# A hybrid attention and state-space layer: token sums and split output weights in spaced steps, V copies beside the second half's units, unused dense products at the beginning of attention

## The chip, the cores and the metric

The kernel runs on one core of one Trainium2 chip. The time is device time in microseconds (us) of that core; the median of the runs counts. A profiled execution has a time of its own, which stands beside them.

## The reference, cut to what matters

One decoder layer on 2048 tokens of width 1024, all in float32. The input x is projected by one large matrix into q, k, v, two gates z, the state-space branch's xbc and dt. Then come two branches, a concatenation, one output projection and a layer norm:

```
proj = einsum('bsd,de->bse', x, w_in)
q, k, v, z_att, z_ssm, xbc, dt_raw = split(proj, SPLITS)
o1, l1 = dilated_window_attention(q, k, v, slopes, 1)     # 16 heads of 64, window of 128 steps
o2, l2 = dilated_window_attention(q, k, v, slopes, 4)
o3, l3 = dilated_window_attention(q, k, v, slopes, 16)
wts = softmax(stack([l1, l2, l3]))
y_att = rms_norm((wts[0]*o1 + wts[1]*o2 + wts[2]*o3) * silu(z_att), att_norm_g)
xbc = silu(causal_depthwise_conv(xbc, conv_w, conv_b))
dt = softplus(dt_raw + dt_bias)
y = ssd_chunked(xs, dt, -exp(a_log), b, c) + d_skip * xs  # chunks of 128
y_ssm = rms_norm(y * silu(z_ssm), ssm_norm_g)
out = einsum('bse,ed->bsd', concat([y_att, y_ssm]), w_out)
x = layer_norm(alpha * x + out, ln_g, ln_b)
```

## The kernel before, in words

Products in full precision are made of three matmuls in a faster 32-bit format: each operand is split into a high part (a cast, on ACT) and a remainder (a subtraction, on DVE or POOL), and high x high, high x low and low x high are added up in PSUM.

**Stage 1, to about 209 us** (lines 126 to 218): v and dt are projected for all tokens, and x is split. In the same loop the sums of token blocks for the first half of the tokens are made, and the upper eight of the sixteen row blocks of the output weights are split and stored in DRAM (`d_wo`).

**Stage 2, to about 1248 us** (lines 220 to 723): all other projections, by a Strassen-like scheme of seven products where eight would be needed. A *job* makes 256 columns of the projection for one half of the tokens (1024): 10 jobs on the first half (jobs 0 to 9, states and gates of the state-space branch), 22 on the second half (jobs 10 to 31), and 12 on the first half again (jobs 32 to 43, q, k and the attention gate). The order is the list `jobs` (lines 605 to 612). A job is seven *steps*, and a step is one product: twelve matmuls of 128x128 by 512 columns (`mm` in `products`, lines 305 to 352). So there are 308 steps; step 7m + s is step s of job m.

A product needs a token tile and a weight tile. The seven token tiles (`LEFT`, line 85) are blocks of x or sums of blocks; they lie in DRAM as `d_T` and are loaded, when the token half changes, by fourteen transfers of 1 MB on POOL's queue (`token_side`, lines 225 to 236), one tile after each step of the job before, as each old tile comes free. The weight tiles of the next job are made in each job: loads on ACT's queue (`column_load`), sums on DVE (line 258), casts on ACT (line 265), remainders on POOL (line 266). Results leave PSUM by copies on ACT (`keep`, line 319) and additions on DVE (`put`, line 327).

The order on PE, DVE, ACT and POOL is the order of the program (`manual_schedule`, line 650): each of these engines does its instructions one after the other, and an instruction that waits holds up all behind it. SP issues transfers. Work that belongs to no job is put into steps by hand: `later` maps a step's number to functions, `after(n, f)` adds one n steps on, and `flush` runs them after each step's product (lines 294 to 303). Put there are, among others:

- the token sums of the second half (`sums_load`, `sums_part`, lines 95 to 112): for each of four row groups k, two loads of 128x1024 from x, and four parts. A part is one subtraction on DVE (line 108), a cast on ACT (line 110), the remainder on DVE (line 111) and a store on SP's queue (line 112), all in one step. In job 1 + k they stand in steps 1 to 4. The buffers: two `st`, two `to`.
- the lower eight row blocks of the output weights, in halves (`wout_load` and `split_w`, lines 115 to 123 and 654 to 659): sixteen loads on ACT's queue at steps 35 to 55, three steps later the cast on ACT (line 117) and the remainder on DVE (line 118) in one step, two steps later the store on POOL's queue (line 119).
- 32 copies of V from DRAM to DRAM in the order of the two larger dilations (`copy_v`, line 496), on POOL's queue, 512 KB each: 13 at steps 3 to 51, 19 at steps 77 to 149, every fourth step.
- softplus and decays of dt (`decays`, lines 440 to 491), in pieces after jobs 1, 2 and 3; the first of them is a chain of small DVE instructions (lines 453 to 474).
- the convolution (three long DVE instructions per tile, line 416) in jobs 10 to 22, and from step 157 on the 32 units of the state-space scan (lines 503 to 601).

**Stage 3, to about 1765 us** (lines 726 to 1133): attention, eight pairs of heads. A pair has 24 units (three dilations d, four blocks, two halves). A unit is 12 score matmuls with 64 rows (line 816), a fused add-and-minimum on DVE (line 824), exponentials on ACT (line 832), transposes on PE (line 845) copied by DVE (line 847), and value matmuls (line 865). PE does the scores of unit i, the transposes of unit i-2 and the values of unit i-3 in one pass of the loop at line 1079. In the dilation that comes first (d = 0, units 0 to 7) and in the first block of the next (units 8 and 9), a unit has 128 keys for each query block instead of 256. The queries for the other dilations are permuted on POOL (`permute`, lines 773 to 787).

**Stage 4** (lines 1134 to 1181): output projection and layer norm.

Of the kernel before, what the change touches and what calls it, by code (L numbers as in the profile page):

```python
# [9 lines left out]
F32 = mybir.dt.float32  # L10
# [18 lines left out]
def hybrid_layer(ctx, tc, xT, xc, w52, wv, convw, convb, dtb, alog, dskp, gcol, wout,  # L29
# [56 lines left out]
    with ExitStack() as c1:  # L86
# [8 lines left out]
        def sums_load(pool, p, k):  # L95

            r = [pool.tile([128, 1024], F32, name="st", bufs=4 if p == 0 else 2) for _ in range(2)]
            for h in range(2):
                kk = k + 4 * h
                nc.sync.dma_start(r[h], xT[kk * 128:(kk + 1) * 128, p * 1024:(p + 1) * 1024])  # L100
            return r

        def sums_part(pool, p, k, r, c):
# [5 lines left out]
            t = pool.tile([128, 2, 512], F32R, name="to", bufs=6 if p == 0 else 2)  # L109
            nc.scalar.copy(t[:, 0], o)  # L110
            nc.vector.tensor_tensor(t[:, 1], o, t[:, 0].bitcast(F32), op=OP.subtract)
            nc.sync.dma_start(dap(d_T[p, nm], k * 512, [[2048, 128], [128 * 2048, 2], [1, 512]]), t.bitcast(F32))


        def split_w(e, hf, raw, t, store=True):
# [3 lines left out]
            put_w = lambda queue: queue.dma_start(d_wo[e][:, :, hf * 512:hf * 512 + 512], t.bitcast(F32))  # L119
            if store:  # L120
                put_w(nc.sync)
            else:
                after(2, lambda: put_w(nc.gpsimd))


        with tc.tile_pool(name="ts", bufs=1, reuse_waits="tile") as ts, \
# [57 lines left out]
            for pc in range(4):  # L184
# [19 lines left out]
                if 0 < pc < 3:  # L204
                    for k in (2 * pc - 2, 2 * pc - 1):
                        r = sums_load(ts, 0, k)
                        for c in range(4):
                            sums_part(ts, 0, k, r, c)
# [441 lines left out]
        with tc.manual_schedule(engines={E.PE, E.DVE, E.Activation, E.Pool}):  # L650
# [599 lines left out]
```

## Time and profile before

| | us |
|---|---|
| median of 3 runs | 2175.16 |
| lowest, highest run | 2175.14, 2181.51 |
| the profiled execution's own time | 2171.41 |
| its span, first to last instruction | 2169.6 |
| mean granted TensorE clock in it | 0.972 |

A page of the profile lists the busy time of each engine, the granted clock and the DMA load over the span, and groups of instructions by line. Views of the trace answer closer questions: how busy each engine was between two times, who waited for whom, and which instructions ran in a window, with the idle time before each and what ended it. PE is TensorE's matmuls, PEld its weight loads, DVE VectorE, ACT ScalarE, POOL GpSimd, SP SyncE. L310 is line 310 of the kernel. In rows of windows, the columns are: window, its length, then busy time and number of instructions of each engine, then granted clock, mean busy share of the 16 DMA engines, and GB/s. The profile's shares are averages over four unlike stages, so what a part is worth is read from its own stretch.

### The profile page before, as it was taken

Reading aid. Unit: us, or ns where it says so; the run is one execution under the profiler, and the core shown is the slowest. Engines: PE = TensorE matmul, PEld = TensorE weight load, DVE = VectorE, ACT = ScalarE, POOL = GpSimd, SP = SyncE. Lnnn points to the kernel's source line nnn. Section 1 sums busy time; section 2 is a strip of 40 time slices with the busy share of each in tenths; the row PEclk is TensorE's granted clock in tenths of the full one; section 3 lists DMA queues with packets and bytes.
Section 4 is the critical chain, followed back from the end, with each engine's and each line's share of the span. In section 5 each row is a group of like instructions: output and inputs, shape, how many; then the busy total and the mean of one; then the engine's idle time right before and its main releaser. Section 6 shows DMA issues by size and latency. Waiting matters only on the chain.

```text
span 2169.6 us, 38851 instructions
## 1 busy us (share of the span) xinstructions
PE 2048.0 (94%) x13824; PEld 1703.7 (79%) x13824; DVE 1394.1 (64%) x3145; ACT 1154.4 (53%) x3007; POOL 1092.5 (50%) x899
## 2 busy tenths in 40 slices
PE   7999998989999999979999999999999977999998
PEld 7998776768887887858888877888878865888886
DVE  3431554548998677835555468888888845655655
ACT  4231444435565677645676468888888841222221
POOL 2122545657886666755555331776666670422222
PEclk9999999989999999999999979999999988999999
DMA  9999778976678888899888853777876799232220
GB/s 330 370 333 338 234 255 281 326 279 213 204 231 293 310 318 302 296 389 298 269 276 286 302 203 88 217 222 220 245 212 185 213 366 286 95 105 84 96 83 29
DMA packets 260801, 525.26 MB, mean 242 GB/s; under 512 B 43712, under 2 KB 122688, under 8 KB 244608
## 3 DMA queue, kind: packets, MB, share of 16 engines
q1 hardware_dynamic: 181984, 255.37, 36.9%
q0 software_dynamic: 35280, 184.30, 24.1%
q10 hardware_dynamic: 43344, 83.12, 11.7%
q8 instruction: 109, 1.79, 0.3%
q14 instruction: 84, 0.69, 0.1%
HBM read 346.15 MB, written 193.33 MB: 249 GB/s over the span
## 4 chain that ended last, share of the span: by engine, by line
PE 47%; DMA 8%; DVE 5%; ACT 3%; issue 3%; POOL 2%; ACTq 0%; SPq 0%; POOLq 0%; DVEq 0%
PE S L816 7%; PE N L865 7%; PE T L845 6%; PE S L1025 4%; PE S L1027 3%; PE S L1026 3%; PE pp L310 3%; PE pp L314 3%; PE pp L312 3%; PE T L1025 2%; PE T L1026 2%; PE T L1027 2%; DMA TT3l<-d_T0T 1%; DVE P L824 1%; ACT P L832 1%
## 5 line engine op out<-in xcount | busy, mean ns | idle before, releaser
L266 POOL TENSOR_TENSOR w<-wr,w 128x512 fp32r<-128x512 f32 x231 | 357.2, 1562 | 177.5 <-ACT w L265 146.5
L832 ACT ACTIVATE P<-P,st 128x256 f32<-128x256 f32 (+1 forms) x768 | 345.1, 451 | 96.6 <-DVE st L824 96.2
L824 DVE CUSTOM_DVE_ANT_0 P<-S,tb 128x256 f32<-128x256 f32 (+1 forms) x768 | 235.4, 362 | 81.3 <-PE S L816 47.2
L319 ACT COPY ev<-pp 128x512 f32<-128x512 f32 x176 | 102.2, 581 | 184.9 <-PE pp L314 123.4
L847 DVE COPY PT<-T 128x512 f32<-128x512 f32 (+1 forms) x304 | 196.5, 677 | 1.3 <-PE T L845 1.3
L845 PE MATMUL T<-ident,P 128*128 128x128 f32 x1200 | 178.8, 286 | 6.0 <-DVE PT L847 6.0
L865 PE MATMUL N<-PT,v 128*64 128x128 f32 x2400 | 176.5, 284 | 0.0
L265 ACT CAST w<-wr 128x512 fp32r<-128x512 f32 x231 | 137.9, 618 | 52.5 <-DVE wr L258 35.8
L865 PEld LDWEIGHTS N<-PT,v 128*64 128x64 f32 x2400 | 129.2, 138 | 33.2 <-issue 22.6
L258 DVE TENSOR_TENSOR wr<-wr 128x512 f32<-128x512 f32 x132 | 145.0, 1099 | 15.6 <-DMA wr<-w 12.5
L845 PEld LDWEIGHTS T<-ident,P 128*128 128x128 f32 x1200 | 129.8, 142 | 30.3 <-DVE PT L847 7.4
L932 POOL TENSOR_TENSOR wb<-num,wb 128x2048 f32<-128x2048 f32 x21 | 96.4, 4591 | 98.1 <-ACT P L832 57.8
L832 ACT ACTIVATION_READ_ACCUMULATOR P<-P,st 128x1 f32 x768 | 143.9, 187 | 0.0
L327 DVE TENSOR_TENSOR ev<-pp,ev 128x512 f32<-128x512 f32 x152 | 100.6, 682 | 53.5 <-PE pp L314 45.2
L816 PE MATMUL S<-kh,qp 64*128 64x256 f32 (+1 forms) x1024 | 126.6, 306 | 0.0
L1002 DVE TENSOR_REDUCE tb<-P 128x128 f32<-128x1024 f32 x32 | 64.0, 2000 | 85.2 <-PE N L1031 49.2
L416 DVE SCALAR_TENSOR_TENSOR acc<-U,cw,acc 128x2048 f32<-128x2048 f32 x36 | 105.2, 2922 | 3.2 <-ACT acc L413 2.8
L816 PEld LDWEIGHTS S<-kh,qp 64*128 64x128 f32 x1024 | 88.9, 188 | 22.0 <-issue 20.9
L367 DVE SCALAR_TENSOR_TENSOR ev<-ev 128x512 f32<-128x512 f32 x64 | 64.2, 1015 | 64.3 <-ACT ev L366 64.2
L150 PE MATMUL pp<-vh,xh 128*128 128x256 f32 (+1 forms) x320 | 90.2, 289 | 15.4 <-ACT xh L173 15.4
L143 POOL TENSOR_TENSOR vl<-vraw,vh 128x256 fp32r<-128x256 f32 (+1 forms) x32 | 29.7, 933 | 130.5 <-ACT vh L142 125.7
L1064 POOL TENSOR_TENSOR kh<-kh,wb 128x1024 f32<-128x1024 f32 x8 | 19.2, 2398 | 142.6 <-DVE kh L1063 142.6
(368 smaller groups left out, 6135.2 us busy)
## 6 DMA issues: line engine op xcount, KB each, us to landing
wr<-w ACTq DMA_DIRECT2D x157, 256.0 KB
v<-d_v POOLq DMA_DIRECT2D x24, 1024.0 KB, 7.0
wb<-d_wd SPq DMA_DIRECT2D x48, 512.0 KB
d_wc<-w SPq DMA_DIRECT2D x44, 512.0 KB
w<-d_wc POOLq DMA_DIRECT2D x44, 512.0 KB, 6.2
csb<-d_cs ACTq DMA_DIRECT2D x32, 512.0 KB
st<-xT SPq DMA_DIRECT2D x31, 512.0 KB
d_v<-vt SPq DMA_DIRECT2D x16, 512.0 KB
```

Source lines behind the costliest of these rows:

```text
L258: tt = lambda o, a, b, op=OP.subtract: nc.vector.tensor_tensor(q[o], q[a], q[b], op=op)
L265: nc.scalar.copy(t[:, 0], q[nm])
L266: nc.gpsimd.tensor_tensor(t[:, 1], q[nm], t[:, 0].bitcast(F32), op=OP.subtract)
L816: nc.tensor.matmul(ov(sp[h][:, 256 * b:256 * b + w]), A["q"][d][x][hr, blk], kv(A["k"][y][hr]), start=(m == 0), stop=(m == 2))
L824: nc.vector.tensor_tensor_reduce(P[:, h, b, 256 - w:256], sp[h][:, c0:c0 + w], tab[:, h, tab.shape[2] - w:], 1.0, 3.0e38, OP.add, OP.min, ...
L832: nc.scalar.activation(p, p, AF.Exp, bias=stat(A, 0, d, h, blk), scale=-1.0, accum_out=stat(A, 1, d, h, blk))
L845: nc.tensor.transpose(tp[:, h, b], P[:, h, b, 128 * which:128 * which + 128], ident)
L847: nc.vector.tensor_copy(pt[:, :, bl[0]:2], tp[:, :, bl[0]:2])
L865: nc.tensor.matmul(nm[64 * h:64 * h + 64, bq * 128:bq * 128 + 128], v[:, k, 64 * h:64 * h + 64], pts[which][:, h, b], start=(f or not whic ...
L1025: nc.tensor.matmul(ps, uh[:, e, :], wh, start=(e == 0), stop=False)
L1026: nc.tensor.matmul(ps, uh[:, e, :], wl, start=False, stop=False)
L1027: nc.tensor.matmul(ps, ul[:, e, :], wh, start=False, stop=(e == 7))
```

## The change

- Token sums of the second half: `sums_load` and `sums_part` keep only stage 1's use. A new `token_sums(k, b)` puts every single operation into a step of its own: for group k, with b = 7 + 8k, four loads of 128x512 at steps b-7, b-3, b-2 and b, and for part c the subtraction at b + 2c, the cast at b + 2c + 1, the remainder and the store at b + 2c + 2. The buffers: five `st` of half the size, two `to`. The last store is at step 39, and the pool is closed after job 5 instead of job 4.
- Split output weights: `w_steps` puts load, cast, remainder and store of each of the sixteen halves at steps c, c + 3, c + 4 and c + 5, with c from 42 to 62. The queues are the same. `woraw` has four buffers instead of three.
- The 32 copies of V stand at steps 73, 76, ... 166, every third step.
- `warm`: after the scores of each of the first four units of attention, eight matmuls of 128x128 by 512 columns on a tile of k, into a PSUM tile of the transposes' ring. Nothing reads the result.

```diff
-        def sums_load(pool, p, k):
+        def sums_load(pool, k):
...
+        put = lambda n, f: later.setdefault(n, []).append(f)
+
+        def token_sums(k, b):
+            R = {}
+            def load(nm, h, q):
+                R[nm] = sums.tile([128, 512], F32, name="st", bufs=5)
+                kk = k + 4 * h
+                nc.sync.dma_start(R[nm], xT[kk * 128:(kk + 1) * 128, 1024 + 512 * q:1536 + 512 * q])
+            for n, x in ((-7, ("11", 0, 0)), (-3, ("12", 0, 1)), (-2, ("22", 1, 1)), (0, ("21", 1, 0))):
+                put(max(b + n, 0), lambda x=x: load(*x))
+            for c, (nm, o, a, d) in enumerate((("T1", "11", "12", "11"), ("T3", "12", "22", "12"),
+                                               ("T2", "22", "22", "11"), ("T4", "21", "22", "21"))):
+                t = []
+                def high(o=o, t=t):
+                    t.append(sums.tile([128, 2, 512], F32R, name="to", bufs=2))
+                    nc.scalar.copy(t[0][:, 0], R[o])
+                def low(o=o, t=t, nm=nm):
+                    nc.vector.tensor_tensor(t[0][:, 1], R[o], t[0][:, 0].bitcast(F32), op=OP.subtract)
+                    nc.sync.dma_start(dap(d_T[1, nm], k * 512, [[2048, 128], [128 * 2048, 2], [1, 512]]),
+                                      t[0].bitcast(F32))
+                put(b + 2 * c, lambda o=o, a=a, d=d: nc.vector.tensor_tensor(R[o], R[a], R[d], op=OP.subtract))
+                put(b + 2 * c + 1, high)
+                put(b + 2 * c + 2, low)
...
-            put_w = lambda queue: queue.dma_start(d_wo[e][:, :, hf * 512:hf * 512 + 512], t.bitcast(F32))
-            if store:
-                put_w(nc.sync)
-            else:
-                after(2, lambda: put_w(nc.gpsimd))
+            nc.sync.dma_start(d_wo[e][:, :, hf * 512:hf * 512 + 512], t.bitcast(F32))
+        def w_steps(e, hf, c):
+            R = []
+            g = gc[:, e:e + 1]
+            def load():
+                R.append(sums.tile([128, 512], F32, name="woraw", bufs=4))
+                nc.scalar.dma_start(R[0], wout[e * 128:e * 128 + 128, hf * 512:hf * 512 + 512])
+            def high():
+                R.append(sums.tile([128, 2, 512], F32R, name="wot", bufs=4))
+                nc.scalar.activation(R[1][:, 0], R[0], AF.Copy, scale=g)
+            def low():
+                nc.vector.scalar_tensor_tensor(R[1][:, 1], R[0], g, R[1][:, 0].bitcast(F32), op0=OP.mult,
+                                               op1=OP.subtract)
+            def store():
+                nc.gpsimd.dma_start(d_wo[e][:, :, hf * 512:hf * 512 + 512], R[1].bitcast(F32))
+            for n, f in ((0, load), (3, high), (4, low), (5, store)):
+                put(c + n, f)
...
-            def wout_load(j):
-                raw = sums.tile([128, 512], F32, name="woraw", bufs=3)
-                nc.scalar.dma_start(raw, wout[j // 2 * 128:j // 2 * 128 + 128, j % 2 * 512:j % 2 * 512 + 512])
-                after(3, lambda: split_w(j // 2, j % 2, raw, sums.tile([128, 2, 512], F32R, name="wot", bufs=4), False))
             for j in range(16):
-                later.setdefault(35 + 4 * j // 3, []).append(lambda j=j: wout_load(16 + j))
+                w_steps(8 + j // 2, j % 2, 42 + 4 * j // 3)
+            for k in range(4):
+                token_sums(k, 7 + 8 * k)
             for j in range(32):
-                later.setdefault(4 * j + (3 if j < 13 else 25), []).append(lambda j=j: copy_v(1 + j // 16, j % 16))
+                put(73 + 3 * j, lambda j=j: copy_v(1 + j // 16, j % 16))
...
-            raws = {0: sums_load(sums, 1, 0)}
...
-                if 1 <= m < 5:
-                    for c in range(4):
-                        after(1 + c, lambda c=c, k=m - 1: sums_part(sums, 1, k, raws[k], c))
-                    if m < 4:
-                        after(5, lambda k=m: raws.__setitem__(k, sums_load(sums, 1, k)))
...
-                if m == 4:
+                if m == 5:
                     sub.close()
...
+        def warm(A):
+            ps = psT.tile([128, 512], F32, name="T")
+            x = A["k"][0]
+            for n in range(8):
+                nc.tensor.matmul(ps, x[:, 0, :], x[:, 4:8, :].rearrange("p r j -> p (r j)"), start=True, stop=True)
...
                     pts[i] = scores(pairs[pr], d, qd, half)
+                    if i < 4:
+                        warm(pairs[0])
```

More of the change, by code (lines that the diff above doesn't have):

```diff
@@ L93, in hybrid_layer, with sums_part @@
         dsk = sm.tile([128, 8], F32, name="dsk")
-        def sums_load(pool, p, k):
-            r = [pool.tile([128, 1024], F32, name="st", bufs=4 if p == 0 else 2) for _ in range(2)]
+        def sums_load(pool, k):
+            r = [pool.tile([128, 1024], F32, name="st", bufs=4) for _ in range(2)]
             for h in range(2):
                 kk = k + 4 * h
-                nc.sync.dma_start(r[h], xT[kk * 128:(kk + 1) * 128, p * 1024:(p + 1) * 1024])
+                nc.sync.dma_start(r[h], xT[kk * 128:(kk + 1) * 128, 0:1024])
             return r
-        def sums_part(pool, p, k, r, c):
+        def sums_part(pool, k, r, c):
             b11, b12, b21, b22 = r[0][:, 0:512], r[0][:, 512:1024], r[1][:, 0:512], r[1][:, 512:1024]
@@ L205, in hybrid_layer @@
                     for k in (2 * pc - 2, 2 * pc - 1):
-                        r = sums_load(ts, 0, k)
+                        r = sums_load(ts, k)
                         for c in range(4):
-                            sums_part(ts, 0, k, r, c)
+                            sums_part(ts, k, r, c)
                 if pc in (1, 2):
```

6 lines of the change are left out of this document (3 added, 3 removed).

## Prediction

> **What bounds the kernel now.** The page first: PE is busy for almost the whole span, so time is gained only where PE stands still or runs slowly. Steps and jobs are counted as in the section on the kernel. The stretches below are cut at the start of job 0, of job 10 (the change of token half), of jobs 11, 22 and 23, of attention, and of its pair 1.
>
> ```profile
> span 2169.6 us, 38851 instructions
> PE 2048.0 (94%) x13824; PEld 1703.7 (79%) x13824; DVE 1394.1 (64%) x3145; ACT 1154.4 (53%) x3007; POOL 1092.5 (50%) x899
> ```
> ```profile
> core 0: us, PE busy (x) PEld busy (x) DVE busy (x) ACT busy (x) POOL busy (x), PEclk, DMA share, GB/s
> 209.40:428.90 219.50, 200.42 (x847) 162.83 (x848) 124.94 (x158) 98.63 (x172) 122.87 (x120) 0.95 0.80 271
> 428.90:466.70 37.80, 26.44 (x86) 18.92 (x85) 5.61 (x10) 7.59 (x12) 15.28 (x19) 0.82 1.01 379
> 466.70:679.00 212.30, 211.08 (x926) 172.99 (x925) 195.90 (x144) 121.58 (x194) 172.41 (x135) 1.00 0.69 215
> 679.00:706.40 27.40, 22.44 (x86) 17.65 (x85) 22.26 (x19) 12.84 (x21) 14.45 (x8) 0.88 0.92 318
> ...
> 1248.40:1319.90 71.50, 68.63 (x676) 55.57 (x675) 50.73 (x227) 51.69 (x203) 23.51 (x37) 0.81 0.47 165
> ```
>
> The same view for line 310 alone, which has four matmuls in a step, dates the losses of the first half:
>
> ```profile
> 209.40:263.20 53.80, 30.17 (x76) 14.72 (x77) 0.97 0.81 261
> 263.20:282.20 19.00, 5.88 (x12) 2.80 (x13) 0.82 0.62 213
> ...
> 312.40:331.90 19.50, 8.49 (x20) 3.99 (x19) 0.91 0.64 227
> 331.90:356.50 24.60, 14.13 (x36) 6.93 (x37) 1.00 0.78 254
> 356.50:404.40 47.90, 22.97 (x57) 10.89 (x57) 0.93 0.86 297
> ```
>
> Nine undisturbed steps take 24.6 us, so a fed step costs 2.73 us (and one of its 12 products 0.228). The 70 steps of jobs 0 to 9 would then take 191.3; they take 219.5, 28.2 more. The second row has 3 steps in 19.0 (10.8 lost), the third 5 in 19.5 (5.8), the last 14 in 47.9 (9.7); the first, 19 in 53.8, loses 1.9, most of it the very first weight tile. Job 10 loses 37.8 - 19.1 = 18.7, jobs 11 to 21 lose 212.3 - 210.4 = 1.9, job 22 loses 8.3.
>
> Who stops PE in jobs 0 to 9? The view of waits names ACT's copies out of PSUM. The timeline of ACT (brackets: idle before, and what ended it) and of DVE shows what stood in front of these copies:
>
> ```profile
> PE pp L310 <- ACT ev L319: 18.6, 6, 7.6
> ```
> ```profile
> 268.18 0.62 ACT L110 CAST to<-st 128x512 fp32r<-128x512 f32 x1 [8.27 <-DVE st L108]
> 272.62 0.62 ACT L110 CAST to<-st 128x512 fp32r<-128x512 f32 x1 [3.30 <-DVE st L108]
> 273.14 0.58 ACT L319 COPY ev<-pp 128x512 f32<-128x512 f32 x1
> ...
> 299.67 0.62 ACT L110 CAST to<-st 128x512 fp32r<-128x512 f32 x1 [5.31 <-DMA d_T1T<-to]
> 325.54 0.62 ACT L110 CAST to<-st 128x512 fp32r<-128x512 f32 x1 [7.23 <-DMA d_T1T<-to]
> 370.26 0.72 ACT L117 ACTIVATE wot<-woraw,gc 128x512 fp32r<-128x512 f32 x1 [3.73 <-DMA d_wo<-wot]
> ```
> ```profile
> 252.24 0.41 DVE L453 TENSOR_TENSOR xr<-xr,dtbt 128x256 f32<-128x256 f32 x1
> 267.12 0.43 DVE L474 TENSOR_TENSOR adt<-dts,al 128x256 f32<-128x256 f32 x1
> 267.46 0.68 DVE L108 TENSOR_TENSOR st<-st 128x512 f32<-128x512 f32 x1
> ```
>
> ACT works in order. In the first two rows its cast of a token sum waits for a subtraction that stands on DVE behind the whole softplus chain (252.2 to 267.5); in the two casts of line 110 that follow it waits until an older sum has been stored; in the last row until an older split weight has been stored. These are the places that the spaced steps touch.
>
> **The change, part by part.**
>
> *Token sums and weights (jobs 0 to 9).* The number of casts, subtractions and stores is the same. What moves is the distance: subtraction, cast, remainder and store were in one step, now they stand one step (2.73 us) apart, and a sum's buffer is taken again three steps after its store was issued. The 13 V copies of these steps go away. Stretch by stretch: the softplus chain stays on DVE, begun after step 13 as now. The cast of group 1 at step 16 still waits for the subtraction of step 15, which comes after 267.5 plus one remainder and itself, 1.4, so at about 268.9; then cast, one weight cast, and ACT copies for PE at about 270.3, where now the copy begins only at 273.1 because a second cast sat in front of it. I keep 6 of the 10.8. The waits for stores should nearly go (1 of 5.8 kept), and of the weights' 9.7 I keep 1.8, since cast and remainder no longer wait on each other back to back. Saving 4.8 + 4.8 + 7.9 = **17.5 us**. Bounds: 8 (only the weights' part) and 24 (all but the first tile and 2 us).
>
> A remainder risk is DVE itself:
>
> ```profile
> 306.29 5.90 DVE L108 TENSOR_TENSOR st<-st 128x512 f32<-128x512 f32 x1
> 306.60 5.03 POOL L266 TENSOR_TENSOR w<-wr,w 128x512 fp32r<-128x512 f32 x4
> ```
>
> One subtraction of usually 0.68 lasted 5.90 while POOL ran four tensor operations beside it. The Trainium skill (SBUF — State Buffer, Who interferes with whom) says that a VectorE instruction with two SBUF inputs and a GpSimd instruction that reads SBUF lock each other out; the trace agrees, and by that rule a distance of one step does not cover such a block.
>
> *The reload of the second half (job 10).* Split weights are now loaded at steps 42 to 62 and stored on POOL's queue five steps later, at 47 to 67. The fourteen 1 MB loads of job 10's token tiles are issued on the same queue from step 63 on. Until now the last store was issued at 409.0, ahead of them:
>
> ```profile
> L119 POOL DMA_DIRECT2D d_wo<-wot x16: 677/695/822, 348.7 to 409.0; - x16
> d_wo<-wot POOLq DMA_DIRECT2D x16, 512.0 KB, 6.5
> q0 software_dynamic: 35280, 184.30, 24.1%
> L496 POOL DMA_DIRECT2D d_v<-d_v x32: 514/572/835, 224.2 to 676.8; - x32
> ```
>
> Job 10 is bound by these transfers (DMA share 1.01, 379 GB/s). Four stores (steps 63, 64, 65, 67) now lie among them: 4 x 0.524 MB at 379 GB/s is **+5.5 us**; bounds 0 and 10 (the upper one also for the convolution's first buffers, which now take the memory of weight buffers whose stores lie in that queue). Two V copies (73, 76) queue behind the loads and cost job 10 nothing, at most 3.
>
> *V copies.* From queue 0, 184.3 MB took 24.1% of 2169.6 us, so a copy of 0.524 MB takes 1.5 us of all 16 DMA engines, and 0.6 us of POOL to issue. Behind a copy on POOL stand the weight remainders (line 266) that PE needs one job later. In jobs 11 to 21 there are 25 copies for 19: 9 us of DMA on a stretch with share 0.69, 3.6 us of POOL where 40 of 212 are free. I take +1, bounds 0 and 5. The last five (154 to 166) fall into jobs 22 and 23, where no copy was, where the DMA share is 0.92 already and ACT waits for stores of its own results:
>
> ```profile
> 688.34 0.58 ACT L319 COPY ev<-pp 128x512 f32<-128x512 f32 x1 [4.52 <-DMA d_kh<-ev]
> ```
>
> Five copies are 7.5 us of DMA; I take **+3**, bounds 0 and 8.
>
> *Unused products at the start of attention.* Pair 0 takes 71.5 us with a clock of 0.81. The score matmuls (12 to a unit) and then all engines:
>
> ```profile
> 1258.80:1280.20 21.40, 9.26 (x72) 8.13 (x72) 0.50 0.20 74
> 1328.30:1342.20 13.90, 6.19 (x84) 5.21 (x84) 1.00 0.36 96
> 1248.40:1258.80 10.40, 7.53 (x65) 5.92 (x64) 6.31 (x36) 8.57 (x34) 10.00 (x15) 0.78 1.00 342
> 1258.80:1280.20 21.40, 21.40 (x146) 16.78 (x144) 9.75 (x54) 11.70 (x53) 2.44 (x5) 0.50 0.20 74
> 1258.96 2.28 POOL L784 CAST qp<-ql 128x512 fp32r<-128x512 f32 x4
> ```
>
> Units 4 to 9 take 3.57 us each at half clock, the same units of pair 1 1.99 at full clock: 6 x 1.58 = 9.5, and unit 10 another 0.5. DMA is nearly idle, and POOL is done with the permuted queries at 1261.2, so nothing else is late there. The price: 32 products of 0.228 are 7.3 us on PE in the first four units, where PE has 10.4 - 7.5 = 2.9 idle; those units get rid of their own half-clock part (clock 0.78 over 10.4 us is 4.6 us at half, so 2.3). So +2.1, and in all **-7.9**; bounds -10 and +12 (below). That the clock stays granted I take from pair 1: the same small products keep full clock there once it is granted, and the clock is lost in pair 0 while PE waits. The Trainium skill (TensorE: Matmul & The Clock Gate, Part 1) says that one busy window of about 3.4 us brings full clock. By that, units 4 to 10 would be fast already and this part would cost 2.1 instead of saving 7.9. The trace disagrees: 21.4 us without a gap at 0.50. So the rule gets no share of the chances.
>
> **Sum.** -17.5 + 5.5 + 1 + 3 - 7.9 = -15.9. The profiled execution's own time is 2171.4 (span 2169.6 and 1.8 around it), 3.8 under the median 2175.2 of the runs; it becomes 2155.5, the median **2159.3**.
>
> **Rivals.** (1) *The clock falls all the same*, because the gaps between the four groups are too long. Then 32 products cost 0.456 each, 14.6 - 2.9 = +11.7 for -7.9: 2159.3 + 19.6 = 2178.9, no change. For it: four small groups with waits between. Against: each group is denser than anything in that stretch. 8%.
> (2) *Spacing buys little*: the chain on DVE and SP's late stores delay the casts at any distance that short, and only 4 of 17.5 come: 2172.8, no change. For it: 8.27 of the waits has the softplus chain behind it, which stays. Against: 9.7 us hang on weights, far from that chain. 11%.
> (3) *Slower: POOL is held by its own queue.* Issuing there can stop until an older transfer has landed:
>
> ```profile
> 433.67 0.53 POOL L233 DMA_DIRECT2D TT4l<-d_T1T  x1 [3.91 <-DMA TT1l<-d_T1T]
> ```
>
> Were each of the 30 copies from job 11 on held so for 3 us, POOL would stand 90 us, and it has 53 free in jobs 11 to 22 (239.7 less 172.4 and 14.5): 37 us late on weights, 2159.3 + 37 = 2196. It decides once eight transfers are outstanding on POOL's queue when a copy is issued (in this row T4's load waits for the one eight places ahead of it). Against: there fourteen loads came in a row, now a copy comes every third step, 8.2 us, and takes 1.5 us of transfer. 10%.
> (4) *Better*: with the copies gone, jobs 0 to 9 lose only 4 and jobs 22 and 23 nothing: 2150. 9%.
>
> **Numbers.** Forecast 62%. About 0.3% (6.5 us) is what a measurement of this kernel can tell from no change. Faster: forecast and (4), 0.71. Same: (1) and (2), 0.19. Slower: (3), 0.10. Range 2146 to 2178: below it lies the forecast with nearly all best bounds, above it (1) and (3), 18%.
>
> **What would show it.** Jobs 0 to 9 in about 202 us instead of 219.5, ACT's casts without waits on stores, one remaining stall near step 20. Job 10 at 43 instead of 37.8, all on DMA waits. Jobs 11 to 21 within 214, job 22 near 30. Pair 0 at about 64 us instead of 71.5, with clock 1.00 after 1250. It would be wrong if the stretch 209 to 429 stays over 212, if clock 0.50 stands in pair 0, or if POOL waits for landings at the copies.

## The result, and the profile after

The changed kernel takes 2194.24 us at the median of 6 runs (2186.44 to 2199.24), the kernel before, beside it, 2176.22 (2173.27 to 2181.51): a ratio of 1.0072 [1.0057, 1.0087]. It is slower by 0.7%, where 0.7% faster was forecast, and it lies outside the range. The profiled execution took 2199.24 us, 5 above its median, so its span exaggerates a little: 27.7 us over that of before, where the medians differ by 18.0.

```profile
span 2197.3 us, 38933 instructions
PE 2054.4 (93%) x13856; PEld 1705.9 (78%) x13856; DVE 1395.1 (63%) x3145; ACT 1153.8 (53%) x3007; POOL 1082.2 (49%) x899
```

PE has 6 us more work (the 32 unused products) and 27.7 us more span: what was lost was lost standing or at a lower clock. The busy windows, cut at the same points as before (starts of job 0, 10, 11, 22, 23, 32, then pair 0 of attention), say where:

```profile
core 0: us, PE busy (x) PEld busy (x) DVE busy (x) ACT busy (x) POOL busy (x), PEclk, DMA share, GB/s
210.30:410.70 200.40, 195.17 (x846) 160.59 (x847) 124.76 (x158) 98.00 (x172) 117.36 (x104) 0.98 0.76 252
410.70:453.20 42.50, 27.36 (x85) 18.96 (x84) 5.52 (x10) 7.65 (x12) 19.38 (x25) 0.80 1.04 398
453.20:695.70 242.50, 220.05 (x925) 176.81 (x924) 202.11 (x144) 119.97 (x191) 162.08 (x139) 0.96 0.64 202
695.70:725.50 29.80, 21.11 (x85) 16.68 (x84) 20.47 (x19) 14.50 (x24) 15.05 (x11) 0.89 0.95 316
725.50:960.00 234.50, 222.89 (x1183) 183.39 (x1182) 162.65 (x238) 157.51 (x318) 154.88 (x123) 0.98 0.87 305
1279.68:1347.10 67.42, 65.69 (x708) 53.08 (x707) 50.29 (x227) 51.45 (x203) 23.55 (x37) 0.97 0.49 176
```

Jobs 22 to 31 together, in the same view of the kernel before:

```profile
679.00:929.90 250.90, 240.61 (x1267) 197.81 (x1266) 184.22 (x257) 172.03 (x342) 169.14 (x128) 0.99 0.88 310
```

| stretch | before | after | difference | forecast |
|---|---|---|---|---|
| to job 0 | 209.4 | 210.3 | +0.9 | 0 |
| jobs 0 to 9 | 219.5 | 200.4 | -19.1 | -17.5 |
| job 10 | 37.8 | 42.5 | +4.7 | +5.5 |
| jobs 11 to 21 | 212.3 | 242.5 | **+30.2** | +1 |
| jobs 22 to 31 | 250.9 | 264.3 | **+13.4** | +3 |
| jobs 32 to 43 | 318.5 | 319.6 | +1.1 | 0 |
| pair 0 | 71.5 | 67.4 | -4.1 | -7.9 |
| the rest | 849.7 | 850.2 | +0.5 | 0 |

Two rows hold most of the miss, 39.6 of the 43.6 us between the forecast change of the span (-15.9) and the measured one (+27.7), and both are stretches to which V copies were moved. In jobs 11 to 21 the DMA share fell from 0.69 to 0.64 although there are six copies more: the engines' bandwidth did not run out. POOL is no busier than before (162 us of 242). Something waited. The view of waits for that stretch, lines that bear on the path to PE; first before:

```profile
POOL U L395 <- DMA d_xs<-U: 13.4, 4, 8.1
ACT ev L319 <- POOL w L266: 8.1, 2, 4.9
DVE U L325 <- DMA d_xs<-U: 8.0, 2, 6.2
```

and after (us in total, times, longest; U is line 442, the remainders 313, PE's third product 361):

```profile
ACT ev L366 <- POOL w L313: 31.4, 5, 11.2
DVE U L372 <- DMA d_xs<-U: 21.1, 4, 7.4
POOL U L442 <- DMA d_xs<-U: 18.5, 4, 7.0
PE pp L361 <- POOL w L313: 15.2, 8, 8.9
POOL U L442 <- issue: 12.3, 1, 12.3
PE pp L357 <- ACT ev L366: 7.0, 4, 5.7
ACT ev L366 <- DMA d_ql<-ev: 4.5, 1, 4.5
```

So PE itself waits 15.2 us for remainders of POOL and 7.0 for ACT's copies out of PSUM. `d_xs<-U` is the store of the convolution's results, on SP's queue. There are two buffers U. The load of the next U stands in POOL's queue, and it must wait until the buffer's store has landed. Behind it in POOL's queue stand the weight remainders that PE needs in the next job. One such chain, read from the timelines of SP, POOL, DVE and PE:

```profile
532.09 1.67 SPq L475 DMA_DIRECT2D d_xs<-U  x1
```
```profile
533.11 0.62 POOL L543 DMA_DIRECT2D d_v<-d_v  x1
533.75 2.54 POOL L313 TENSOR_TENSOR w<-wr,w 128x512 fp32r<-128x512 f32 x2
548.61 1.55 POOL L442 DMA_DIRECT2D U<-d_cu  x2 [12.31 <-issue]
...
551.35 2.16 POOL L313 TENSOR_TENSOR w<-wr,w 128x512 fp32r<-128x512 f32 x1
```
```profile
546.46 1.29 DVE L372 TENSOR_TENSOR U<-pp,ev 128x512 f32<-128x512 f32 x2 [7.35 <-DMA d_xs<-U]
```
```profile
553.56 0.80 PE L361 MATMUL pp<-TT2h,w 128*128 128x512 f32 x1 [8.86 <-POOL w L313]
554.16 0.63 PE L357 MATMUL pp<-TT2h,w 128*128 128x512 f32 x1
...
557.57 0.63 PE L361 MATMUL pp<-TT2h,w 128*128 128x512 f32 x1
...
558.93 0.39 PE L357 MATMUL pp<-TB22h,w 128*128 128x512 f32 x1
```

A V copy is issued 1 us after the store. DVE's sum into the buffer is held until 546.46, so the store had taken 14 us; POOL does its first remainder in 15 us at 551.35, and PE stands 8.86 us for it. (The timeline puts POOL's 12.31 us down to "issue"; the view of line 475 counts them among the waits of U's loads for such stores, "POOL U L442: 30.8, 5".) From its issue to the last update of its semaphore in the trace, this store of job 14 takes 14.2 us here and 14.1 in the run with only the copies moved, but 5.3 in the kernel before, 6.0 without copies and 5.8 with copies in small packets (both runs below). After that the products start every 0.427 us instead of every 0.228 until about 558.5: the stall also costs the clock, about 2 us more here. Over the stretch, at 0.96 where it was 1.00, PE is busy for 220.05 us with work that took 211.08 before, so 9.0 of the 30.2 us are slower work and not waiting. The Trainium skill (TensorE: Matmul & The Clock Gate, Part 1) says that an idle window of some 3.4 us halves the clock and a busy one restores it; here the trace agrees, with 8.9 us idle and 4.9 us of half rate.

This chain is job 15. Not all the loss goes this way: the longest wait of PE for ACT, 5.7 us in job 20, stands behind a copy on ACT that waits 4.5 us for the store of another result (`d_ql`, the low part of q).

### The profile page after: what moved, and what is told of

Same layout as the page of the kernel before. It is cut to its first block, busy times and chain, and to the rows that moved or that the text cites. A ratio compares the mean times of both kernels' runs of the same rounds, so it can differ in the third digit from the quotient of the medians.

```text
span 2197.3 us, 38933 instructions
## 1 busy us (share of the span) xinstructions
PE 2054.4 (93%) x13856; PEld 1705.9 (78%) x13856; DVE 1395.1 (63%) x3145; ACT 1153.8 (53%) x3007; POOL 1082.2 (49%) x899
## 3 DMA queue, kind: packets, MB, share of 16 engines
q0 software_dynamic: 35280, 184.30, 23.6%
q10 hardware_dynamic: 43344, 83.12, 11.8%
## 4 chain that ended last, share of the span: by engine, by line
PE 41%; DMA 10%; DVE 5%; ACT 4%; issue 2%; POOL 1%; ACTq 1%; SPq 0%; POOLq 0%; DVEq 0%
PE N L911 6%; PE S L855 6%; PE T L891 5%; PE S L1071 3%; PE S L1073 3%; PE S L1072 3%; PE pp L357 2%; PE pp L359 2%; PE pp L361 2%; DMA zt<-d_zs 2%; PE T L1071 2%; PE T L1072 2%; PE T L1073 2%; ACT P L871 1%; DMA kl<-d_kl 1%
## 5 line engine op out<-in xcount | busy, mean ns | idle before, releaser
L313 POOL TENSOR_TENSOR w<-wr,w 128x512 fp32r<-128x512 f32 x231 | 346.6, 1517 | 180.0 <-ACT w L312 128.7
L911 PEld LDWEIGHTS N<-PT,v 128*64 128x64 f32 x2400 | 127.1, 136 | 32.0 <-issue 22.8
L305 DVE TENSOR_TENSOR wr<-wr 128x512 f32<-128x512 f32 x132 | 138.9, 1052 | 12.2 <-DMA wr<-w 5.6
L978 POOL TENSOR_TENSOR wb<-num,wb 128x2048 f32<-128x2048 f32 x21 | 96.4, 4591 | 97.8 <-DMA wb<-d_wd 71.5
L463 DVE SCALAR_TENSOR_TENSOR acc<-U,cw,acc 128x2048 f32<-128x2048 f32 x36 | 118.1, 3280 | 7.8 <-ACT acc L460 7.4
L198 PE MATMUL pp<-vl,xh 128*128 128x256 f32 (+1 forms) x320 | 90.5, 287 | 0.0
```

What stands on the lines that cost most here:

```text
L305: tt = lambda o, a, b, op=OP.subtract: nc.vector.tensor_tensor(q[o], q[a], q[b], op=op)
L313: nc.gpsimd.tensor_tensor(t[:, 1], q[nm], t[:, 0].bitcast(F32), op=OP.subtract)
L463: return lambda: nc.vector.scalar_tensor_tensor(acc[0], U[:, j:j + 16, :], cw[:, i, j:j + 1], acc[0], op0=OP.mult, op1=OP.add)
L911: nc.tensor.matmul(nm[64 * h:64 * h + 64, bq * 128:bq * 128 + 128], v[:, k, 64 * h:64 * h + 64], pts[which][:, h, b], start=(f or not whic ...
```

## The experiments

They ran in four groups, on three chips, on which the kernel before takes about 2182 us; each ratio is to runs of that kernel on the same chip, so ratios are compared and not times. The lengths of stretches come from one profiled execution each. Undisturbed jobs repeat to 0.1 us between kernels, the sums of a stretch to 3 or 4: jobs 0 to 9 with the new spacing and no copies take 200.4 to 203.2, jobs 22 to 31 without copies 250.5 to 254.5. Nor is the profiled execution always near the median: that of "all in jobs 0 to 9" lies 10.3 us above it, "U loaded by SP" 7.8 and "U wholly off POOL" 6.8 below. So a price read from stretches stands beside the ratios where they differ. Theory A: the V copies beside jobs 11 to 31 are the loss. Its rivals: the late weight stores on POOL's queue, the unused products, and (theory B) a new phase of POOL against DVE in the convolution jobs, which the earlier end of jobs 0 to 9 brings. The table has ratios to the kernel before and stretches in us; "no copies" is the floor to which the copies' cost is counted.

| kernel | ratio, 95% interval | 0-9 | 10 | 11-21 | 22-31 | pair 0 |
|---|---|---|---|---|---|---|
| before | 1 | 219.5 | 37.8 | 212.3 | 250.9 | 71.5 |
| after | 1.0072 [1.0057, 1.0087] | 200.4 | 42.5 | 242.5 | 264.3 | 67.4 |
| copies at old steps | 0.9937 [0.9920, 0.9953] | 207.7 | 42.9 | 216.3 | 253.0 | 67.2 |
| before, copies moved | 1.0068 [1.0053, 1.0083] | 203.4 | 36.6 | 239.9 | 264.1 | 71.7 |
| no unused products | 1.0086 [1.0071, 1.0101] | 202.5 | 41.6 | 241.5 | 260.6 | 72.2 |
| no copies | 0.9912 [0.9895, 0.9930] | 202.1 | 43.3 | 215.1 | 252.6 | 65.1 |
| row packets | 1.0012 [0.9995, 1.0029] | 202.2 | 41.6 | 229.9 | 258.8 | 65.6 |
| third dilation first | 1.0088 [1.0056, 1.0120] | 203.2 | 42.3 | 228.1 | 274.8 | 65.1 |
| every fourth step | 1.0011 [0.9994, 1.0028] | 202.7 | 41.6 | 225.4 | 262.7 | 65.4 |
| all in jobs 0 to 9 | 1.0009 [0.9990, 1.0028] | 222.6 | 47.6 | 217.1 | 253.0 | 65.2 |
| U loaded by SP | 1.0038 [1.0016, 1.0060] | 200.7 | 45.5 | 232.7 | 254.8 | 65.2 |
| row packets, every fourth | 0.9998 [0.9979, 1.0016] | 202.7 | 41.7 | 213.2 | 275.4 | 65.0 |
| row packets, old steps | 0.9928 [0.9900, 0.9955] | 200.5 | 40.9 | 220.6 | 254.5 | 66.9 |
| copies late | 1.0129 [1.0097, 1.0160] | 200.6 | 41.0 | 215.7 | 250.5 | 67.7 |
| U wholly off POOL | 1.0023 [1.0008, 1.0038] | 202.1 | 43.1 | 232.4 | 258.0 | 65.0 |
| last five early | 1.0020 [1.0007, 1.0033] | 202.2 | 41.4 | 241.7 | 250.8 | 67.1 |
| only last five late | 0.9970 [0.9955, 0.9985] | 207.7 | 45.0 | 215.8 | 255.9 | 69.4 |

**The copies back at their old steps**, all else as changed:

```diff
-                put(73 + 3 * j, lambda j=j: copy_v(1 + j // 16, j % 16))
+                put(4 * j + (3 if j < 13 else 25), lambda j=j: copy_v(1 + j // 16, j % 16))
```

> The changed kernel with the 32 V copies at their old steps (3 to 51 and 77 to 149); sums, weights and unused products as changed. Theory A: the copies beside jobs 11 to 31 cost the 43 us that these jobs lost; then jobs 11 to 31 fall back to about 463 us, jobs 0 to 9 stay near 201 to 206, and the time is 2150 to 2160, 0.990 of before. Theory B: the losses come from the new phase of POOL against DVE in the convolution jobs, which the earlier end of jobs 0 to 9 brings, whatever the copies do; then the time stays at 2185 to 2200.

0.9937: the loss is gone and the rest of the change is a gain. Busy windows of jobs 0 to 9 and 11 to 21:

```profile
210.60:418.30 207.70, 199.34 (x847) 163.34 (x847) 125.71 (x158) 98.66 (x172) 125.94 (x115) 0.96 0.80 272
461.20:677.50 216.30, 213.32 (x925) 173.91 (x924) 198.44 (x144) 123.53 (x195) 168.31 (x134) 0.99 0.69 212
```

Spacing sums and weights alone thus saves 11.8 us in jobs 0 to 9.

**Only the copies moved**, in the kernel before:

```diff
-                later.setdefault(4 * j + (3 if j < 13 else 25), []).append(lambda j=j: copy_v(1 + j // 16, j % 16))
+                later.setdefault(73 + 3 * j, []).append(lambda j=j: copy_v(1 + j // 16, j % 16))
```

> The kernel before with nothing changed but the steps of the V copies (73, 76, ... 166). Theory A: jobs 11 to 31 lose about 43 us, jobs 0 to 9 gain 5 to 10 for the missing copies: 2205 to 2215. Theory B: jobs 11 to 31 lose little: 2165 to 2176.

1.0068: this one line makes the whole slowdown. It also saves 16.1 us in jobs 0 to 9, more than the spacing alone; both together save 19.1, so most of the two gains is the same stalls. Job 10, with the weights stored early as before, shows what the late stores cost: 36.6 here, 42.5 with them.

```profile
413.20:449.80 36.60, 26.45 (x85) 18.99 (x84) 5.53 (x10) 7.57 (x12) 16.49 (x21) 0.81 1.05 396
```

**Without the unused products:**

```diff
-                    if i < 4:
-                        warm(pairs[0])
```

> The changed kernel without the unused products at the start of attention. If they are worth what the two traces show in pair 0 (71.5 to 67.4), the time is 4 us longer, 2198, with clock 0.5 over some 27 us of pair 0. Rival: the start of pair 0 costs more with them than the trace of pair 0 shows (its first units took 6.35 and 2.87 us), and without them the time is 2190.

1.0086; its interval overlaps that of the changed kernel (1.0072), so the ratios cannot tell the two apart, and the trace has to. Pair 0 takes 72.2 us again, with units 4 to 9 at half clock, as in the kernel before:

```profile
1285.70:1307.10 21.40, 21.40 (x148) 16.73 (x146) 9.75 (x54) 11.65 (x52) 1.65 (x3) 0.50 0.16 58
```

**No copies.** All three dilations read V in the first one's order, so two of them attend to wrong rows; the loads of V in attention stay as many and as large.

```diff
-            for j in range(32):
-                put(73 + 3 * j, lambda j=j: copy_v(1 + j // 16, j % 16))
...
-            nc.gpsimd.dma_start(v, d_v[d][:, :, pr * 128:pr * 128 + 128].rearrange("b p e -> p b e"))
+            nc.gpsimd.dma_start(v, d_v[0][:, :, pr * 128:pr * 128 + 128].rearrange("b p e -> p b e"))
```

> The changed kernel without any V copy; all three dilations read V in the order of the first, so two of them attend to the wrong rows of V. Theory A: jobs 11 to 31 take 463 us or less, 2145 to 2155. Theory B: as the changed kernel, 2185 to 2200.

0.9912, and jobs 11 to 31 take 467.7 us where after takes 506.8: the copies cost 39.1 us there; by the medians they cost 0.0160, 35 us in all. Theory A is shown, and B falls, since jobs 0 to 9 end as early here (202.1 us). Most of the loss sits in few jobs: job 14 takes 23.5 us instead of 19.0, job 15 30.5, job 19 23.6, job 20 28.7 (21.0 without copies). The DMA share without copies is 0.55, the emptiest stretch of stage 2:

```profile
455.50:670.60 215.10, 211.01 (x926) 173.10 (x925) 198.35 (x144) 121.69 (x194) 161.63 (x116) 1.00 0.55 166
923.20:1240.90 317.70, 303.81 (x1649) 251.02 (x1647) 164.79 (x292) 191.85 (x391) 160.76 (x160) 0.97 0.90 303
```

Next question: what about the copies costs so much, when 19 of them at the old steps, every fourth, cost 1.2 us? Three theories: their density, the size of their packets, their place. In the trace a copy for the second dilation is 8 packets of 64 KB, 2.8 us each, as a rule four at a time, so that it lasts 5 to 8 us; one for the third dilation is 16 packets of 32 KB, 1.7 us each, nearly all at once. The two kinds thus differ in spread as well as in size. The old steps had mostly third-dilation copies beside jobs 11 to 21.

**Row packets**, 4 KB each; the same rows in another order:

```diff
-            nc.gpsimd.dma_start(d_v[d][b], dap(d_v[0], o * D, [[128 * D, (4, 16)[d - 1]], [D, (32, 8)[d - 1]], [1, D]]))
+            n, r = ((4, 32), (16, 8))[d - 1]
+            nc.gpsimd.dma_start(dap(d_v[d], b * 128 * D, [[D, r], [r * D, n], [1, D]]),
+                                dap(d_v[0], o * D, [[D, r], [128 * D, n], [1, D]]))
```

> The changed kernel with each copy of V cut into 128 packets of 4 KB (row by row) where it had 8 of 64 KB or 16 of 32 KB; the same bytes, the same steps, 32 copies. If the size of the packets is the cause (the convolution's results and ScalarE's loads wait behind packets that take 1.7 to 2.8 us each), jobs 11 to 31 lose under 12 of their 43 us, the time is about 0.99 of before, and ScalarE's issues of 4 us disappear. If bytes beside the convolution are the cause, or the number of copies, jobs 11 to 31 lose 35 or more as in the changed kernel, and the time is 1.005 or more.

Between the two: jobs 11 to 31 give back 18.1 of 39.1 (by the medians 0.0060 of 0.0160), and jobs 13 to 15 lose nothing any more; jobs 16 and 20, at 28.9 and 27.9 us, hold most of what is left (21.2 and 21.0 without copies). ScalarE's long issues are gone too. Line 291 (loads of weights, issued on ACT's queue; durations in ns, least, median, most), after and then with row packets:

```profile
L291 ACTq DMA_DIRECT2D wr<-w x157: 334/339/4635, 226.6 to 1238.2; - x157
```
```profile
L291 ACTq DMA_DIRECT2D wr<-w x157: 334/339/1524, 223.9 to 1218.5; - x157
```

So the large packets held the other queues: 4.6 us for an issue that takes 0.34 at the median. The Trainium skill (DMA: Bandwidth & Descriptors, Queues, rings and completion order) says that each DMA engine goes round its queues a whole packet at a time; that agrees with small packets doing less harm.

**The third dilation first:**

```diff
-                put(73 + 3 * j, lambda j=j: copy_v(1 + j // 16, j % 16))
+                put(73 + 3 * j, lambda j=j: copy_v(2 - j // 16, j % 16))
```

> The changed kernel with the two dilations' copies in the other order: 16 packets of 32 KB at steps 73 to 118, 8 packets of 64 KB at 121 to 166. If the large packets are the cause, jobs 13 to 15 lose under 6 us (16 in the changed kernel) and the loss moves to jobs 20 to 27. If any copy beside these jobs costs the same, the losses stay in the jobs where they were (13 to 15, 19 and 20, 22 to 25). Either way the sum may stay near 2194.

With 32 KB packets there, jobs 13 to 15 lose nothing. The loss of 35.2 us moves to jobs 20 to 25, where the 64 KB packets now are (job 20 29.6, job 22 34.3, job 24 30.8). That is the packet theory in jobs 13 to 15. It is not the whole: jobs 17 to 19 have 64 KB packets too and lose only 1.5, and the other theory also had losses in jobs 20 and 22 to 25.

**Every fourth step:**

```diff
-                put(73 + 3 * j, lambda j=j: copy_v(1 + j // 16, j % 16))
+                put(73 + 4 * j, lambda j=j: copy_v(1 + j // 16, j % 16))
```

> The changed kernel with the copies every fourth step (73 to 197) where it was every third. If their density is the cause, jobs 11 to 21 lose 5 us or less, as the kernel before had a copy every fourth step there too, and the time is under 0.995 of before. If the 64 KB packets are the cause, jobs 13 to 16 still lose 10 or more, since these copies now last to step 133, and the sum is above 1.000.

Neither side's number: jobs 13 to 16 lose 5.8 us against undisturbed jobs of 19.0 (3.6 against the floor), jobs 11 to 21 10.3, and jobs 22 to 31, which now have eleven copies, 10.1. At this same spacing the old steps, with mostly smaller packets, lost 1.2. Density and packet size both matter.

**All copies in jobs 0 to 9:**

```diff
-                put(73 + 3 * j, lambda j=j: copy_v(1 + j // 16, j % 16))
+                put(3 + 2 * j, lambda j=j: copy_v(1 + j // 16, j % 16))
```

> The changed kernel with all 32 copies at steps 3 to 65, every second step, beside jobs 0 to 9, whose queue of SyncE also loads weights and stores the sums. If the place beside the convolution is the cause, jobs 11 to 31 run as without copies (215 and 253 us), and jobs 0 to 9 cost what the copies cost there: between 202 and 217 us, a time of 0.991 to 0.998. If copies cost the same wherever they lie, jobs 0 to 10 take 30 to 40 us more and the sum stays at 1.005.

Jobs 11 to 31 run as without copies (470.1), but jobs 0 to 9 cost 20.5 us more, 5.6 over the upper bound of 217, and job 10 4.3 more. This trace is the slowest of ten executions, so these prices are high; by the medians the copies cost 0.0097, 21 us, where they cost 35 beside the second half.

```profile
211.20:433.80 222.60, 202.34 (x846) 163.94 (x847) 134.12 (x156) 97.18 (x170) 131.93 (x133) 0.95 0.86 293
```

**U loaded on SP's queue**, to test the path through POOL:

```diff
-                nc.gpsimd.dma_start(u[:, 3 + tb:19:4, :], d_cu[i][:, tb].rearrange("p (s j) -> p s j", j=NJ))
-            nc.gpsimd.dma_start(u[:, 0, 1:NJ], d_cu[i][:, 1, 3 * NJ:4 * NJ - 1])
+                nc.sync.dma_start(u[:, 3 + tb:19:4, :], d_cu[i][:, tb].rearrange("p (s j) -> p s j", j=NJ))
+            nc.sync.dma_start(u[:, 0, 1:NJ], d_cu[i][:, 1, 3 * NJ:4 * NJ - 1])
```

> The changed kernel with the loads of the convolution's buffers U issued on SyncE's queue, where they were on GpSimd's, in front of the weight remainders. If the path runs through GpSimd's queue (a late store of d_xs holds the load of U, and that holds the remainders behind it), jobs 13 to 15 lose under 6 of their 17 us and jobs 11 to 31 come down by 10 or more. If the late stores stop TensorE by the other way, through VectorE's sums into U, jobs 11 to 31 stay within 5 us of the changed kernel (507).

Jobs 11 to 31 come down by 19.3 us with every copy at the same step and in the same packets. But this is the fastest of eight executions; by the medians the edit gives back 0.0034 of 0.0160, 7 us. The path through POOL is real, and worth between a fifth and a half. Jobs 13 to 15 still lose 9.3, not under 6. The waits say why the test is not clean: a memset of U (line 444) stayed on POOL and now waits in place of the load.

```profile
POOL U L444 <- DMA d_xs<-U: 22.9, 4, 9.9
DVE U L372 <- DMA d_xs<-U: 12.4, 4, 5.6
PE pp L361 <- POOL w L313: 6.3, 3, 3.1
```

**Row packets and every fourth step together** (both edits above):

> The changed kernel with both: 128 packets of 4 KB to a copy, and a copy every fourth step (73 to 197). Each alone took back 18 or 19 of the 39 us by which jobs 11 to 31 exceed the run without copies. If they are two causes, jobs 11 to 31 take 468 to 476 us and the time is 0.992 to 0.996. If both act on the same loss (and the rest comes from the copies' lying beside jobs 22 to 28), jobs 11 to 31 stay at 483 or more and the time is 0.999 or more.

Jobs 11 to 21 take 213.2 us, no more than without copies, and the wait of PE for remainders, 15.2 us in after, no longer appears in the list. So beside the convolution, in jobs 11 to 21, the two causes together are the whole loss. But the copies now last to step 197, and jobs 22 to 31 lose 22.8:

```profile
454.50:667.70 213.20, 211.41 (x925) 174.49 (x924) 197.78 (x144) 123.58 (x195) 171.83 (x135) 0.99 0.69 214
667.70:943.10 275.40, 246.96 (x1268) 202.02 (x1267) 182.22 (x257) 170.47 (x339) 172.44 (x140) 0.96 0.88 307
```

Eleven copies at 2.1 us each, in a stretch whose DMA share is 0.88: there the place costs, and row packets do not help. They may even harm: at the same steps the old packets lost 10.1, in one execution each.

**Row packets at the old steps:**

> The changed kernel with the copies at their old steps (3 to 51, and 77 to 149 every fourth), in row packets of 4 KB. With the old packets this order lost 8 us against the run without copies, 5.6 of it in jobs 0 to 9 and 1.5 in jobs 11 to 31. If the 64 KB packets are what costs in jobs 0 to 9, these take 202 to 204 us and the time is 0.991 to 0.993; if the bytes are, 207 us and 0.994.

0.9928, the best version with its output whole; it cannot be told from the old steps with the old packets (0.9937). Jobs 0 to 9 take 200.5 us: 13 copies there are free in row packets and cost 5.6 in the old ones. Jobs 11 to 21 have 5.5 over the floor, which I can't explain: the same packets at nearly the same steps cost nothing in the run before this.

**Copies late**, beside jobs 32 to 41:

```diff
-                put(73 + 3 * j, lambda j=j: copy_v(1 + j // 16, j % 16))
+                put(227 + 2 * j, lambda j=j: copy_v(1 + j // 16, j % 16))
```

> The changed kernel with the copies at steps 227 to 289, every second step, beside jobs 32 to 41, where there is no convolution and no result of the second half is stored but where the scan loads and stores. If it is the convolution and the stores of jobs 13 to 25 that the copies disturb, jobs 11 to 31 run as without copies (468 us), jobs 32 to 43 lose under 10 us, and the time is 0.992 to 0.996. If 32 copies cost some 35 us wherever they lie close together, jobs 32 to 43 take 350 and the time is 1.006.

Slower still, and more than either theory gave. Jobs 32 to 43 take 368.4 us for 317.7 without copies: 50.7 for 32 copies, 1.6 us each, which is their 1.5 us of DMA time from queue 0. Where the DMA share is already 0.90, a copy costs what it moves.

```profile
919.00:1287.40 368.40, 318.64 (x1651) 259.16 (x1649) 159.60 (x292) 194.42 (x392) 179.94 (x193) 0.94 0.87 305
```

**U wholly off POOL's queue**: the loads on SP, as above, and the zeros by a DMA on SP.

```diff
-            nc.gpsimd.memset(u[:, 0:3, 0:1], 0.0)
+            nc.sync.dma_start(u[:, 0:3, 0:1], zer)
...
+        zer = sm.tile([128, 3, 1], F32, name="zer")
+        nc.gpsimd.memset(zer, 0.0)
```

> The changed kernel with everything that writes U before the sums taken off GpSimd's queue: its loads issued on SyncE, and the zeros of its first column by a small DMA on SyncE from a tile of zeros (with the loads alone moved, the memset stayed on GpSimd and still waited 22.9 us for stores of d_xs). If GpSimd's queue is the main way by which late stores stop TensorE, jobs 13 to 16 lose under 6 us (20 in the changed kernel, 14 with the loads alone moved) and jobs 11 to 31 take under 480. If VectorE's sums into U, which wait for the same stores, carry as much, jobs 11 to 31 stay at 484 or more.

Jobs 13 to 16 lose 6.8 us, near the first theory's bound, but jobs 11 to 31 stay at 490.4, the second theory's side: what is gained in these jobs is lost again in jobs 12, 17 and 18. POOL waits for no store any more; it waits for ACT's casts instead, and PE for ACT:

```profile
POOL w L313 <- ACT w L312: 52.1, 19, 6.9
PE pp L357 <- ACT ev L366: 7.7, 4, 3.5
PE pp L361 <- POOL w L313: 3.6, 6, 1.1
PE pp L357 <- ACT w L312: 3.2, 2, 2.9
```

(POOL's wait for casts is 33.8 in after and 34.8 without copies.) So POOL's queue is one of the ways: without it PE waits 3.6 us for remainders instead of 15.2. It is worth 16.4 of the 39.1 us by the stretches of this fast execution, and 0.0049 of 0.0160, 11 us, by the medians. The rest comes through ACT at least, as the rows show; what DVE's sums add was not tested apart.

**The last five copies early**; only these five moved, to steps 3 to 35:

```diff
-                put(73 + 3 * j, lambda j=j: copy_v(1 + j // 16, j % 16))
+                put(73 + 3 * j if j < 27 else 3 + 8 * (j - 27), lambda j=j: copy_v(1 + j // 16, j % 16))
```

> The changed kernel with the last five copies (steps 154 to 166, jobs 22 and 23) put at steps 3 to 35 instead. If these five cost what the forecast gave them, jobs 22 to 31 come down by 3 to 264 less 3, 261; if the 13 us by which jobs 22 to 31 grew are theirs, to 253; jobs 11 to 21 stay at 240 either way. If the loss there is carried over from buffers that came late in jobs 20 and 21, jobs 22 to 31 stay above 258.

**Only the last five late**; the others at their old steps:

```diff
-                put(73 + 3 * j, lambda j=j: copy_v(1 + j // 16, j % 16))
+                put(73 + 3 * j if j >= 27 else 4 * j + (3 if j < 13 else 25), lambda j=j: copy_v(1 + j // 16, j % 16))
```

> The changed kernel with 27 copies at their old steps and only the last five at 154 to 166. Jobs 11 to 21 take 212 to 217 as with all at the old steps. If five copies beside jobs 22 and 23 cost 3, jobs 22 to 31 take 256; if they cost 13, 266. With copies at the old steps these jobs took 253.

Jobs 22 to 31 of the first and of the second:

```profile
695.30:946.10 250.80, 240.08 (x1268) 197.79 (x1267) 178.92 (x256) 169.28 (x338) 169.46 (x129) 0.99 0.89 311
```
```profile
679.90:935.80 255.90, 241.03 (x1267) 198.50 (x1266) 184.93 (x256) 170.09 (x338) 167.64 (x133) 0.98 0.90 313
```

Taken from the changed kernel, the five give back 13.5 us. Added to a kernel whose jobs 11 to 21 run freely, they cost 2.9, no more than the spread of this stretch. By the traces the same transfers cost several times as much behind a stretch that is already late. By the medians it is 0.0052 against 0.0033, 11 us against 7, which the intervals do not tell apart: that they cost more there is likely, how much more is not shown.

## Why the prediction was wrong

*Jobs 0 to 9* (-17.5): right in size, -19.1, with one cast still waiting 8.87 us for its subtraction at 270.28, as foreseen. Wrong in its account: the 13 copies that go away had no price of their own, and taking away either the copies (-16.1) or the close spacing (-11.8) removes most of the same stalls. That the sum came out right is luck in part.

*Job 10* (+5.5): right, +4.7, on DMA waits; with the old weight stores it takes 36.6.

*V copies in jobs 11 to 21*, "I take +1, bounds 0 and 5": this is the step that failed, by 29 us. It compared 9 us of DMA time with a share of 0.69 and 3.6 us of POOL with 40 free. Both averages were true and neither decides. What decides is how late a store lands that something waits for. The chain shown is one 1 MB store of the convolution (14 us, above): two buffers and the orders of POOL's and DVE's queues carry its lateness to PE within a job. In job 20 it is the store of q, by way of ACT. The prediction named the weight remainders behind the copy on POOL, but not the load of U in the same queue, which waits for that store; the trace of before showed that wait, 13.4 us in 4 cases, one of 8.1. It also counted 25 copies for 19 as six more of the same. Of the 19, three were of the second dilation, with 64 KB packets; of the 25 it is fourteen, and these come every third step.

*The last five copies*, "+3, bounds 0 and 8": mis-sized as a term that stands alone. By themselves they cost 2.9, about what was put down; behind the late jobs it was 13.5 (both by single traces).

*Unused products* (-7.9): the mechanism was right. The clock is granted for good after the first units, and units 4 to 9 take 1.99 us instead of 3.57:

```profile
1279.68:1290.00 10.32, 8.59 (x54) 6.61 (x54) 3.33 (x19) 5.82 (x19) 9.95 (x15) 0.83 0.96 336
1290.00:1311.00 21.00, 21.00 (x225) 16.58 (x224) 14.18 (x81) 15.74 (x73) 3.04 (x6) 1.00 0.22 80
```

The price was too low: the first four units take 16.4 us instead of 10.4, +6.0 where 2.1 was put down. In all -4.1 here, and 65.0 to 69.4 us for pair 0 in the other kernels with these products, against 71.5 to 72.2 without.

*Rivals.* The third, POOL held by its own queue, gave 2196 and the measured 2194.24 is near it, but not by its mechanism. POOL was not held at the copies:

```profile
L543 POOL DMA_DIRECT2D d_v<-d_v x32: 514/574/635, 439.0 to 751.5; - x32
```

All 32 issues took their usual 0.6 us. POOL was held at the load of U, by a transfer of another queue. What is shown by this: the copies make the loss (the run with only the copies moved and the run without copies settle that), size and density of packets beside the convolution make it there, and POOL's queue carries between a fifth and a half. That DMA load makes it beside jobs 32 to 41 fits the price, 1.6 us for 1.5 of transfer; in jobs 22 to 31 it is argued only, since the same eleven copies lost 10.1 in the old packets and 22.8 in rows. What stays open: how the rest divides between ACT's held issues, ACT's copies that wait for stores, and DVE's sums into U, and which slows a store more, the packet's size or that the packets of a second-dilation copy run four at a time; row packets change both.

## What to carry to other kernels

Price an added transfer not by the mean DMA share of the stretch but by the transfers beside it whose landing something waits for: look up in the waits who waits for a store, which in-order queue that waiter stands in, and what stands behind it. Do not take it that two such costs add up: a term found in an undisturbed stretch may hold only as long as the stretch stays so (2.9 against 13.5 us in the traces here). Compare the medians too before a price is read from one trace: here single executions lay up to 10 us off. And test a composite change by its parts: here one line turned a gain of 0.6% into a loss of 0.7%.

## What the runs showed of the hardware

A DRAM-to-DRAM copy in 64 KB packets held issues on another engine's queue: 4.6 us at most for a load that takes 0.34 to issue, 1.5 with 4 KB packets. A copy of four runs of 128 KB went as eight packets of 64 KB, as a rule four at a time (2.8 us each); a copy of sixteen runs of 32 KB went nearly all at once (1.7 us each). Where the DMA engines are nearly full (share 0.90 without copies), a 512 KB copy cost 1.6 us of kernel time; at share 0.55, every fourth step, 19 or 20 copies cost between nothing and 10 us together in four runs (213.2 to 225.4 us for jobs 11 to 21, where none takes 215.1). And 21.4 us of unbroken work in small products at half clock did not bring the full clock, while products of 512 columns among the first units brought it within the first unit (6.35 us in the changed kernel, granted 1.00 from then on).
